# Zero products first, held loads and another x layout at the start of a decoder trunk

## The chip, the cores and the metric

The kernel runs on one core of a Trainium2 chip. The metric is device time in microseconds (us). A run's time is that of the whole execution; the profile of one execution also gives the span from its first to its last instruction.

## The reference

A trunk of two decoder layers in float32 on an input x of 256 tokens by 1024 channels. The first layer mixes tokens with a gated MLP, the second with block attention; each is followed by a gated MLP with a causal convolution, and each of the four sublayers ends in `x <- LayerNorm(alpha * x + f(x))`. What matters here is the head of the first sublayer:

```python
def chunked_gmlp(x, w_in, ln_g, ln_b, w_s, b_s, w_out):
    z = jax.nn.gelu(x @ w_in)          # (256, 1024) @ (1024, 2048)
    u, v = jnp.split(z, 2, axis=-1)
    v = layer_norm(v, ln_g, ln_b)
    ...
    return (u * sv.reshape(B, S, GMLP_WIDTH)) @ w_out
```

The kernel begins with the v half: x times the right 1024 columns of `w_in`, which are stored as the input `a_v`.

## The kernel before, in words

Every product of matrices is made of products on TensorE of a 128x128 stationary operand with up to 512 moving columns, in the type fp32r. To keep float32 accuracy each operand is split in two: `hi`, the value rounded to fp32r (ScalarE, ACT, line 338), and `lo`, the rest (VectorE, DVE, line 344). Each product is then three: hi by hi, hi by lo, lo by hi (`rows_step`, line 553; the instruction is at line 326).

All weights come through one queue of loads that SyncE (SP) issues in order (`load`, line 353; the DMA instruction is at line 355). They are cut into chunks of 128 partitions by 2048 columns, 1 MB each, which land in two buffers in turn (`raws`). A chunk covers two k tiles of 128 rows of the weight. `prep` (line 385) loads a chunk and splits it into `whi` and `wlo` tiles of 1024 columns, five chunks ahead of TensorE. A chunk can only be loaded into a buffer when both splits of the chunk two places earlier have read it, so the third chunk waits for the splits of the first.

At the start there is nothing to run ahead of, so the first loads are cut up and their order on SP is set by ranks (`FIRST`, line 382; `XFIRST`, line 383). The program's tiles are called raw_85 and raw_86 in the listing of instructions. The pieces, with the names that this text uses:

| rank | load | size | name here |
|---|---|---|---|
| 0 | a_v chunk 0, columns 0 to 511 | 256 KB | W0a |
| 1 | x, k tile 0 | 128 KB | x0 |
| 2 | a_v chunk 0, columns 512 to 1023 | 256 KB | W0b |
| 3 | x, k tile 1 | 128 KB | x1 |
| 4 | a_v chunk 0, columns 1024 to 2047 | 512 KB | W0c |
| 5 | x, k tiles 2 and 3 | 256 KB | x23 |
| 6, 7 | a_v chunk 1, its two halves | 512 KB each | W1a, W1b |
| 8 | x, k tiles 4 to 7 | 512 KB | x47 |
| none | a_v chunks 2 and 3 | 1 MB each | W2, W3 |
| none | LayerNorm rows for v | 1 MB | lnrow |
| none | a_u chunk 0, the u half's first weights | 1 MB | U0 |

W0a to W0c hold k tiles 0 (W0a, W0b) and 1 (W0c); W1 holds 2 and 3, W2 holds 4 and 5, W3 holds 6 and 7. x is stored transposed, `xT`, with 128 partitions (`load_xt`, line 433); in its rows the token half t stands outside the k tile, so a load of n k tiles moves two pieces of n times 512 bytes per partition.

The v products (`gmlp`, line 641) go over k tiles 0 to 3 for both token halves and then over k tiles 4 to 7 for the first half and the second. A k tile for one token half is two column halves of 512, each with its own PSUM bank, with three products each. So the first four k tiles are 48 products, and the 49th and 50th are the first two that need W2: one with its `whi`, one with its `wlo`.

The order of all instructions is worked out when the program is built: operations are recorded, `Plan.emit` (line 122) gives each a due time from its followers, simulates the engines with estimated costs and writes each engine's stream out by the simulated start. TensorE's main stream keeps the recorded order. What a load waits for is put in by the framework: a buffer's last readers and writers.

Of the kernel before, what the change touches and what calls it, by code (L numbers as in the profile page):

```python
# [11 lines left out]
F32 = mybir.dt.float32  # L12
# [6 lines left out]
P = 128  # L19
D = 1024  # L20
S = 256
DEPTH = 2
KT = D // P
FFN = 2816
FT = FFN // P
NT = S // P
# [9 lines left out]
HALF = 512  # L36
CH = 2048
SUB = 1024
# [7 lines left out]
T1_WAITS = (2600, 3300, 4000, 4700)  # L46
REST = 25000, 9000, 25000
AHEAD = 12000


class Buf:
# [164 lines left out]
def flat(ap):  # L216
    n = 1
    for d in ap.shape[1:]:
        n *= d
    return n  # L220
# [3 lines left out]
def trunk_kernel(ctx: ExitStack, tc: tile.TileContext, a: dict, out: bass.AP):  # L224
    nc = tc.nc
    plan = Plan()
    sb = ctx.enter_context(tc.tile_pool(name="sb", bufs=1))
# [9 lines left out]
    raws = Ring(tiles("raw", RAWS, CH))  # L237
# [9 lines left out]
    rr = sb.tile([P, 2 * FT * S], F32R, name="rr")  # L247
# [28 lines left out]
    state = {"age": 0, "next": 0}  # L276

    def taken(i, long):
        old = bank_of[i][1]
# [34 lines left out]
                bank_of[i] = (bank_of[i][0], b, False)  # L314


    def mms(seq, r, w, fill=False):

        ns = 0.0
        for o, l, x, _, _ in seq:  # L320
            n = flat(x)
            ns += max(107.0, n / 2.4) + 2.5 if l.dtype == F32R else (218.0 if n <= P else n / 0.6 + 5)

        def emit():
            for o, l, x, start, stop in seq:
                nc.tensor.matmul(o, l, x, start=start, stop=stop)  # L326
        plan.op("pe", ns, emit, r, w, fill)

# [24 lines left out]
    def load(o, src, w, r=(), nbytes=None, rank=None):  # L353
        nbytes = nbytes or flat(o) * P * 4
        plan.op("sp", nbytes / 360.0, lambda: nc.sync.dma_start(o, src), r, w, nbytes=nbytes, rank=rank)  # L355

    def split(hi, lo, src, psum=False, by="act"):

# [21 lines left out]


    FIRST = {0: [(0, 512, 0), (512, 1024, 2), (1024, 2048, 4)], 1: [(0, 1024, 6), (1024, 2048, 7)]}
    XFIRST = ((0, 1, 1), (1, 1, 3), (2, 2, 5), (4, 4, 8))

    def prep(i):
        name, c = stream[i]
        raw = raws.new()
        cuts = FIRST.get(i, [(0, CH, None)])
        for s, e, rank in cuts:
            load(raw.ap[:, s:e], a[name][c, :, s:e], [(raw, range(s // 256, e // 256))], rank=rank)  # L390
# [15 lines left out]
    def sub(name, c, s):  # L406
        return chunks[where[name, c]][s]
# [18 lines left out]
    def xt_view(b):  # L426
        return b.ap

    xh, xl = xt_new()
    xT32 = place("ff", HALF, KT * S)  # L430
    xv32 = xT32.ap.rearrange("p (t k c) -> p t k c", t=NT, k=KT)

    def load_xt(k, n, rank):
        load(xv32[:, :, k:k + n, :], a["xT"][:, :, k:k + n, :], [(xT32, [(t, j) for t in range(NT) for j in range(k, k + n)])],
             rank=rank)
# [13 lines left out]
    def ln_rows(i):  # L449
        b = rowring.new()  # L450
        src = a["lnrow"]
        load(b.ap, bass.AP(tensor=src.tensor, offset=src.offset + i * 2 * D, ap=[[0, P], [1, 2 * D]]), [b])
        return b, b.ap.rearrange("p (a d) -> p a d", a=2)

    def load_mixer():
# [94 lines left out]
            plan.later(wait, lambda k0=k0: turn(k0))  # L550


    def rows_step(pieces, hk, lk, r, hi, lo, first, last):

        for o, n, b in pieces:
            parts = range(o // 256, (o + n) // 256)
            mms([(b.ap[:, :n], x, w.ap[:, o:o + n], first and j == 0, last and j == 2)
                 for j, (x, w) in enumerate([(hk, hi), (hk, lo), (lk, hi)])], r + [(hi, parts), (lo, parts)], [b])
        plan.tick()

    def cols_times(b, h, l, hi, lo):
# [21 lines left out]
    def project_out(name, nk, at, xold, li, rows_i):  # L583
# [23 lines left out]
        for t in range(NT):  # L607
# [33 lines left out]
    def gmlp():  # L641
        at = xt_at(xh, xl)
        pieces = [[(o, HALF, bank(True)) for o in (0, HALF)] for _ in range(NT)]
        order = [(k, t) for k in range(4) for t in range(NT)] + [(k, t) for t in range(NT) for k in range(4, KT)]
        v = []
        for k, t in order:
            rows_step(pieces[t], *at(k, t), *sub("a_v", k // 2, k % 2), k == 0, k == KT - 1)
            if t == NT - 1 and k % 2:
                spent("a_v", k // 2)
            if (k, t) == (3, NT - 1):  # L650
                rows = ln_rows(0)
                ws, bs = load_mixer()
            if k == KT - 1:
                vt = place("ff", HALF + t * D, D)
                for o, n, b in pieces[t]:
                    act(vt.ap[:, o:o + n], b.ap, AF.Gelu_apprx_tanh, [b], [(vt, range(o // S, (o + n) // S))],
                        psum=True, table="gelu")
                    done_with(b)
                st, mean, rstd = stats(vt, vt.ap, [(0, HALF), (HALF, HALF)])
                scaled(vt, vt.ap, st, mean, rstd, rows)  # L660
                v.append(vt)
# [17 lines left out]
        for g in range(GROUPS):  # L679
            b = bank()  # L680
# [12 lines left out]
    def conv_up(layer, h, l):  # L693
# [42 lines left out]
        for t in range(NT):  # L736
            b = half()
            for k in range(KT):
# [7 lines left out]
                plan.tick()  # L746
            plan.tick(AHEAD)
            y = yring.new()
# [11 lines left out]
    def moba(h, l, scr):  # L760
# [14 lines left out]
        for ks in (range(5), range(5, KT)):  # L775
            for t in range(NT):
# [4 lines left out]
                if ks[0] == 0 and t == 0:  # L781
                    plan.tick(AHEAD)
                if ks[0]:
# [97 lines left out]
    at = gmlp()  # L881
    h, l = project_out("a_out", KT, at, xtok, 0, 1)
    at = conv_up(0, h, l)
    scr = build_bias(10 * S)
    h, l = project_out("f_dn0", FT, at, xtok, 1, 2)
    at = moba(h, l, scr)
    h, l = project_out("b_o", KT, at, xtok, 2, 3)
    at = conv_up(1, h, l)
    project_out("f_dn1", FT, at, xtok, None, 4)
    plan.tick(1e9)  # L890
    plan.emit()


# [9 lines left out]
def _layout(i):  # L903
    f = lambda v: np.ascontiguousarray(np.asarray(v, dtype=np.float32))
# [65 lines left out]
```

## Time and profile before

| | before |
|---|---|
| time, median of 3 runs | 572.7 us (571.51 to 573.66) |
| time of the profiled execution | 571.2 us |
| its span | 569.5 us |
| TensorE products busy | 556.1 us, 98% of the span |
| VectorE, ScalarE busy | 464.3 us (82%), 359.2 us (63%) |
| moved by DMA | 110.92 MB, mean 195 GB/s |

The profiled execution is 1.7 us longer than its span. PE is TensorE's products, PEld its weight loads, DVE VectorE, ACT ScalarE, POOL GpSimd, SP SyncE. A busy share near 100% on PE says that products were always under way, not at which clock they ran; a product's own time in a row is longer than the distance to the next one, since products overlap in the array. The distance of the starts is what a product costs.

### The profile page before, as it was taken

Reading aid. Unit: us, or ns where it says so; the run is one execution under the profiler, and the core shown is the slowest. Engines: PE = TensorE matmul, PEld = TensorE weight load, DVE = VectorE, ACT = ScalarE, POOL = GpSimd, SP = SyncE. Lnnn points to the kernel's source line nnn. Section 1 sums busy time; section 2 is a strip of 40 time slices with the busy share of each in tenths; the row PEclk is TensorE's granted clock in tenths of the full one; section 3 lists DMA queues with packets and bytes.
Section 4 is the critical chain, followed back from the end, with each engine's and each line's share of the span. In section 5 each row is a group of like instructions: output and inputs, shape, how many; then the busy total and the mean of one; then the engine's idle time right before and its main releaser. Section 6 shows DMA issues by size and latency. Waiting matters only on the chain.

```text
span 569.5 us, 8289 instructions
## 1 busy us (share of the span) xinstructions
PE 556.1 (98%) x3098; PEld 474.9 (83%) x3098; DVE 464.3 (82%) x873; ACT 359.2 (63%) x652; POOL 11.5 (2%) x17
## 2 busy tenths in 40 slices
PE   6999999999999999999999999999999999999994
PEld 4799888888888878888888877788888888888884
DVE  5598989999999997467958988579989999996526
ACT  5555558776777686335578877377777767775300
POOL 0020010000000000001000000010000000000001
PEclk9999999999999999999999999999999999999998
DMA  7897435547554577742665653506455556566302
GB/s 266 330 361 283 181 146 182 189 153 279 171 211 155 216 229 266 270 165 74 222 221 185 194 210 115 222 2 221 156 218 219 201 174 218 195 242 229 147 1 74
DMA packets 20132, 110.92 MB, mean 195 GB/s; under 512 B 2251, under 2 KB 6268, under 8 KB 7676
## 3 DMA queue, kind: packets, MB, share of 16 engines
q1 hardware_dynamic: 20092, 110.39, 54.2%
q8 instruction: 24, 0.39, 0.3%
q14 instruction: 16, 0.13, 0.1%
HBM read 109.31 MB, written 1.07 MB: 194 GB/s over the span
## 4 chain that ended last, share of the span: by engine, by line
PE 95%; DMA 2%; DVE 1%; SPq 0%; ACT 0%; issue 0%; DVEq 0%
PE twos L326 52%; PE bank L326 41%; DMA raw<-in_a_v 2%; PE bank L332 1%; PE twos L332 1%; DVE wlo L344 0%; DVE x L348 0%; SPq L355 0%; ACT whi L338 0%; DVE stat L494 0%; DVEq L966 0%; DVE stat L497 0%; DVE stat L499 0%; DVE xt L344 0%
## 5 line engine op out<-in xcount | busy, mean ns | idle before, releaser
L344 DVE TENSOR_TENSOR wlo<-raw,whi 128x1024 fp32r<-128x1024 f32 (+1 forms) x212 | 228.2, 1099 | 33.7 <-ACT whi L338 32.8
L338 ACT ACTIVATE whi<-raw 128x1024 fp32r<-128x1024 f32 (+1 forms) x212 | 194.8, 954 | 55.1 <-DMA raw<-in_f_dn 21.3
L326 PE MATMUL twos<-xt,whi 128*128 128x512 f32 x640 | 222.2, 394 | 0.0
L326 PE MATMUL twos<-xt,wlo 128*128 128x256 f32 x640 | 177.3, 277 | 0.0
L326 PEld LDWEIGHTS twos<-xt,whi 128*128 128x128 f32 x640 | 120.0, 188 | 27.8
L326 PE MATMUL bank<-whi,rr 128*128 128x512 f32 x432 | 135.5, 391 | 0.0
L326 PEld LDWEIGHTS twos<-xt,wlo 128*128 128x128 f32 x640 | 120.1, 188 | 0.1
L326 PEld LDWEIGHTS bank<-whi,rr 128*128 128x128 f32 x432 | 81.1, 188 | 17.9 <-issue 1.0
L326 PE MATMUL bank<-wlo,rr 128*128 128x512 f32 x216 | 84.0, 389 | 0.0
L326 PE MATMUL bank<-xt,whi 128*128 128x256 f32 (+1 forms) x256 | 71.0, 348 | 0.0
L348 DVE SCALAR_TENSOR_TENSOR ff<-ff,convc 128x254 f32<-128x254 f32 (+1 forms) x160 | 69.6, 478 | 0.3
L338 ACT ACTIVATE ff<-twos 128x512 f32<-128x512 f32 (+1 forms) x56 | 30.8, 565 | 47.9 <-PE twos L326 44.8
L326 PE MATMUL bank<-xt,wlo 128*128 128x256 f32 x192 | 54.0, 281 | 0.0
L326 PEld LDWEIGHTS bank<-xt,whi 128*128 128x128 f32 x256 | 44.0, 190 | 6.8 <-issue 1.0
L326 PEld LDWEIGHTS bank<-wlo,rr 128*128 128x128 f32 x216 | 40.6, 188 | 8.0
L338 ACT ACTIVATE ff<-ff,convc 128x256 f32<-128x256 f32 x80 | 45.6, 592 | 1.9 <-DVE ff L344 1.2
L344 DVE TENSOR_TENSOR ff<-twos,ff 128x512 f32<-128x512 f32 (+1 forms) x48 | 30.9, 645 | 15.3 <-ACT ff L338 13.0
L326 PE MATMUL twos<-whi,xt 128*128 128x512 f32 x128 | 42.1, 396 | 0.0
L338 ACT ACTIVATE ff<-bank,lncol 128x128 f32<-128x128 f32 x48 | 18.8, 458 | 29.1 <-PE bank L332 29.1
L326 PEld LDWEIGHTS bank<-xt,wlo 128*128 128x128 f32 x192 | 36.4, 190 | 0.0
L348 DVE SCALAR_TENSOR_TENSOR x<-x,bank 128x512 f32<-128x512 f32 x16 | 11.0, 686 | 25.0 <-PE bank L326 25.0
L326 PEld LDWEIGHTS twos<-whi,xt 128*128 128x128 f32 x128 | 24.1, 188 | 4.8
(71 smaller groups left out, 489.1 us busy)
## 6 DMA issues: line engine op xcount, KB each, us to landing
raw<-in_f_up SPq DMA_DIRECT2D x44, 1024.0 KB, 4.8
raw<-in_f_dn SPq DMA_DIRECT2D x22, 1024.0 KB, 4.9
raw<-in_b_qk SPq DMA_DIRECT2D x8, 1024.0 KB, 4.9
lnrow<-in_lnrow SPq DMA_DIRECT2D x5, 1024.0 KB, 6.7
raw<-in_a_u SPq DMA_DIRECT2D x4, 1024.0 KB, 5.1
raw<-in_a_out SPq DMA_DIRECT2D x4, 1024.0 KB, 5.0
raw<-in_b_v SPq DMA_DIRECT2D x4, 1024.0 KB, 4.9
raw<-in_b_o SPq DMA_DIRECT2D x4, 1024.0 KB, 5.0
```

The source lines that it names most:

```text
L326: nc.tensor.matmul(o, l, x, start=start, stop=stop)
L332: nc.tensor.transpose(o, x, ident.ap)
L338: plan.op("act", ns, lambda: nc.scalar.activation(o, x, func, **kw), r, w, table=table)
L344: dve(70 + 1.04 * flat(x), lambda: nc.vector.tensor_tensor(o, x, y, op=op), r, w)
L348: lambda: nc.vector.scalar_tensor_tensor(o, x, s, y, op0=op0, op1=op1), r, w)
```

## The change

Four things change, all at the start of the program.

1. After the plan is made and before its instructions are written out, VectorE clears 512 columns of the tile `rr` (which is first used much later), and TensorE multiplies them eight times into a PSUM bank that nothing has used yet (`WARM = 8`).
2. Three loads get a hold: `load` first issues a transfer of 16 numbers from a tile that an earlier load fills into a scratch row. It reads what that load writes, so SP waits for its landing, and everything behind it on SP waits too. x23 is held until W0a has landed, W1b until W0c has, and lnrow until W3 has.
3. `xT` is stored with the k tile outside the token half, so that a load of n k tiles is one piece of n times 1024 bytes per partition.
4. The 12 products of k tile 0 are issued together, sorted by column half first, and inside it hi by hi, x's lo by hi, hi by W's lo, each for both token halves.

```diff
@@ mms @@
         def emit():
-            for o, l, x, start, stop in seq:
+            if into is not None and not ready:
+                return
+
+            for o, l, x, start, stop in seq if into is None else [q for _, _, q in sorted(into, key=lambda q: q[:2])]:
                 nc.tensor.matmul(o, l, x, start=start, stop=stop)
@@ load @@
+        def emit():
+            for j, (i, at) in enumerate(holds):
+                k = state["held"] = state["held"] + 16
+                nc.sync.dma_start(scratch[:, k:k + 16], loaded[i].ap[:1, at:at + 16])
...
+            if len(holds) < 2:
+                nc.sync.dma_start(o, src)
+        plan.op("sp", nbytes / 360.0, emit, r, w, nbytes=nbytes, rank=rank)
@@ prep, load_xt, ln_rows @@
+    HOLD = {5: [(0, 0)], 7: [(0, SUB)]}
+    scratch = sb.tile([1, 128], F32, name="scratch")
+    loaded = {}
...
-    xv32 = xT32.ap.rearrange("p (t k c) -> p t k c", t=NT, k=KT)
+    xv32 = xT32.ap.rearrange("p (k t c) -> p t k c", t=NT, k=KT)
...
+             holds=[(3, 0)] if i == 0 else ())
@@ rows_step @@
+            if into is not None:
+                into += [(i, (0, 2, 1)[j], q) for j, q in enumerate(seq)]
+            mms(seq, r + [(hi, parts), (lo, parts)], [b], into=into, ready=into is not None and len(into) == 12)
@@ trunk_kernel, end @@
+    zeros = rr[:, :HALF]
+    nc.vector.memset(zeros.bitcast(F32), 0.0)
+    for _ in range(WARM):
+        nc.tensor.matmul(banks[-1], zeros[:, :P], zeros, start=True, stop=True)
     plan.emit()
@@ _layout @@
-        "xT": f(x.reshape(NT, P, KT, P).transpose(3, 0, 2, 1)),
+        "xT": f(x.reshape(NT, P, KT, P).transpose(3, 2, 0, 1).reshape(P, KT * S)),
```

SP at the start of the program, before: the loads of the table above in the order of their ranks, then W2, W3, lnrow and U0.

```order
L355 DMA raw_85<-in_a_v 128x512
L355 DMA ff<-in_xT 128x2x128
L355 DMA raw_85<-in_a_v 128x512
L355 DMA ff<-in_xT 128x2x128
L355 DMA raw_85<-in_a_v 128x1024
L355 DMA ff<-in_xT 128x2x256
L355 DMA raw_86<-in_a_v 128x1024 x2
L355 DMA ff<-in_xT 128x2x512 [waits DMAHW0_49]
L355 DMA raw_85<-in_a_v 128x2048 [waits DMAHW2_49,DMAHW4_49,DMAHW1_49,DVE_49]
L355 DMA raw_86<-in_a_v 128x2048 [waits DMAHW7_49,DMAHW6_49,DVE_49]
L355 DMA lnrow_90<-in_lnrow 128x2048 [waits DMAHW3_49]
L355 DMA raw_85<-in_a_u 128x2048 [waits DMAHW1_49,DVE_49]
```

The same place after. DMAHW0 to 7 are eight semaphores that the loads take in turn, so a wait on one is a wait for the landing of an earlier load.

```order
L370 DMA raw_85<-in_a_v 128x1024
L366 DMA scratch<-raw_85 1x16x1 [waits DMAHW0_49]
L370 DMA ff<-in_xT 128x512
L370 DMA raw_86<-in_a_v 128x1024
L366 DMA scratch<-raw_85 1x16x1 [waits DMAHW4_49]
L370 DMA raw_86<-in_a_v 128x1024 [waits DMAHW1_49]
L370 DMA ff<-in_xT 128x1024 [waits DMAHW2_49]
L370 DMA raw_85<-in_a_v 128x2048 [waits DMAHW3_49,DMAHW5_49,DMAHW0_49,DVE_49]
L370 DMA raw_86<-in_a_v 128x2048 [waits DMAHW7_49,DMAHW1_49,DVE_49]
L366 DMA scratch<-raw_86 1x16x1 [waits DMAHW4_49]
L370 DMA lnrow_90<-in_lnrow 128x2048 [waits DMAHW6_49]
L370 DMA raw_85<-in_a_u 128x2048 [waits DMAHW3_49,DVE_49]
```

No load has changed its place among the loads: three tiny transfers stand between them now, each with a wait. W2 also waits for the two tiny transfers that read its buffer (DMAHW5 and 0).

TensorE at the start, before. bank_107 and bank_108 are the column halves of the first token half, bank_109 and bank_110 those of the second; whi_65 and wlo_75 are k tile 0 of the weights.

```order
L326 MATMUL bank_107<-whi_65,xt 128x512
L326 MATMUL bank_107<-wlo_75,xt 128x512
L326 MATMUL bank_107<-whi_65,xt 128x512
L326 MATMUL bank_108<-whi_65,xt 128x512
L326 MATMUL bank_108<-wlo_75,xt 128x512
L326 MATMUL bank_108<-whi_65,xt 128x512
L326 MATMUL bank_109<-whi_65,xt 128x512
```

And after:

```order
L924 MATMUL twos_106<-rr 128x512 x8
L330 MATMUL bank_107<-whi_65,xt 128x512
L330 MATMUL bank_109<-whi_65,xt 128x512
L330 MATMUL bank_107<-whi_65,xt 128x512
L330 MATMUL bank_109<-whi_65,xt 128x512
L330 MATMUL bank_107<-wlo_75,xt 128x512
L330 MATMUL bank_109<-wlo_75,xt 128x512
L330 MATMUL bank_108<-whi_65,xt 128x512
```

Eight products of zeros stand ahead, and the first product with a `wlo` is the fifth instead of the second. Behind k tile 0 TensorE's order is as before, and so are the orders of ScalarE, of GpSimd and, apart from the new clearing at its head, of VectorE.

## Rows read from the trace of the kernel before

**Rows 1.** The page of the profile: busy time, share of the span and instructions of each engine.

```profile
PE 556.1 (98%) x3098; PEld 474.9 (83%) x3098; DVE 464.3 (82%) x873; ACT 359.2 (63%) x652; POOL 11.5 (2%) x17
```

**Rows 2.** The chain that ended last, in order of time: start and length in us, and what it was (the number of instructions behind the x).

```profile
3.15 5.63 DMA raw<-in_a_v
...
8.80 0.64 ACT whi L338
...
10.79 7.21 DMA raw<-in_a_v
...
18.03 1.07 ACT whi L338
...
19.12 1.24 DVE wlo L344
...
20.40 19.62 PE bank L326 x119
...
561.94 0.43 DVE x L348
```

**Rows 3.** TensorE's own waits over the whole span: who waited for whom, us in total, times, longest.

```profile
PE bank L326 <- DVE xt L361: 4.9, 1, 4.9
PE bank L326 <- DVE wlo L344: 0.8, 1, 0.8
```

**Rows 4.** TensorE's products in order of time: start us, us, what, how many in a row, and idle time before. A row of x2 is two products.

```profile
4.92 0.77 PE L326 MATMUL bank<-whi,xt 128*128 128x512 f32 x1 [4.92 <-DVE xt L361]
5.77 0.80 PE L326 MATMUL bank<-wlo,xt 128*128 128x512 f32 x1
...
8.50 0.63 PE L326 MATMUL bank<-wlo,xt 128*128 128x512 f32 x1
...
9.78 0.63 PE L326 MATMUL bank<-wlo,xt 128*128 128x512 f32 x1
10.20 0.98 PE L326 MATMUL bank<-whi,xt 128*128 128x512 f32 x2
11.03 0.40 PE L326 MATMUL bank<-wlo,xt 128*128 128x512 f32 x1
...
17.87 0.39 PE L326 MATMUL bank<-wlo,xt 128*128 128x512 f32 x1
...
18.55 0.39 PE L326 MATMUL bank<-wlo,xt 128*128 128x512 f32 x1
18.78 0.86 PE L326 MATMUL bank<-whi,xt 128*128 128x512 f32 x2
20.40 0.50 PE L326 MATMUL bank<-wlo,xt 128*128 128x512 f32 x1 [0.76 <-DVE wlo L344]
...
31.46 0.28 PE L326 MATMUL bank<-xt,wlo 128*128 128x256 f32 x1
```

**Rows 5.** SP's issues of loads in order of time: start us, us from the first to the end of the last of the row.

```profile
0.80 0.38 SPq L355 DMA_DIRECT2D raw<-in_a_v  x1
...
3.79 0.55 SPq L355 DMA_DIRECT2D ff<-in_xT  x1
4.38 1.07 SPq L355 DMA_DIRECT2D raw<-in_a_v  x2
...
10.79 3.79 SPq L355 DMA_DIRECT2D raw<-in_a_v  x2
14.63 0.43 SPq L355 DMA_DIRECT2D lnrow<-in_lnrow  x1
```

**Rows 6.** Five stretches of the start: length, busy time of each engine with its instructions, granted clock, share of the DMA engines' time, GB/s.

```profile
1.80:5.00 3.20, 0.08 (x1) 0.11 (x1) 0.45 (x3) 0.91 (x2) 0.00 (x0) 1.00 0.70 211
5.00:8.80 3.80, 3.72 (x8) 2.63 (x9) 2.10 (x6) 1.14 (x3) 0.00 (x0) 1.00 0.82 252
8.80:13.50 4.70, 4.70 (x17) 3.71 (x17) 3.83 (x7) 4.07 (x8) 0.00 (x0) 1.00 1.03 393
13.50:18.00 4.50, 4.50 (x22) 3.72 (x21) 1.99 (x4) 1.15 (x2) 0.00 (x0) 1.00 0.96 333
18.00:20.50 2.50, 1.74 (x8) 0.92 (x6) 1.38 (x2) 2.01 (x2) 0.00 (x0) 1.00 1.04 436
```

**Rows 7.** The same view of the rest of the span.

```profile
20.40:561.90 541.50, 541.50 (x3049) 463.92 (x3049) 450.49 (x843) 348.87 (x635) 9.88 (x10) 1.00 0.54 193
```

**Rows 8.** The DMA view of the first 12 us: GB/s in 40 slices of 0.3 us, and one kind of load with its size and its median time from issue to landing.

```profile
GB/s 0 0 0 0 0 0 130 184 179 196 174 299 357 249 230 179 118 207 282 358 348 294 229 254 113 195 212 260 287 375 393 413 437 423 437 376 423 396 376 430
...
raw<-in_a_v SPq DMA_DIRECT2D x2, 256.0 KB, 3.4
```

**Rows 9.** VectorE in order of time, in the same columns as rows 4.

```profile
0.87 0.06 DVE L421 MEMSET nhalf<- 128x1 f32 x1 [0.87 <-PEq L963]
...
5.03 0.68 DVE L344 TENSOR_TENSOR wlo<-raw,whi 128x512 fp32r<-128x512 f32 x1
...
27.38 2.36 DVE L344 TENSOR_TENSOR wlo<-raw,whi 128x1024 fp32r<-128x1024 f32 x2 [0.75 <-ACT whi L338]
...
34.64 0.74 DVE L348 SCALAR_TENSOR_TENSOR ff<-ff,stat,lnrow 128x512 f32<-128x512 f32 x1
```

**Rows 10.** ScalarE in order of time.

```profile
4.21 0.63 ACT L338 ACTIVATE whi<-raw 128x512 fp32r<-128x512 f32 x1 [2.13 <-DMA raw<-in_a_v]
...
26.29 2.01 ACT L338 ACTIVATE whi<-raw 128x1024 fp32r<-128x1024 f32 x2 [0.38 <-DMA raw<-in_a_u]
```

More of the change, by code (lines that the diff above doesn't have):

```diff
@@ L48 @@
 AHEAD = 12000
+WARM = 8
 class Buf:
@@ L275, in trunk_kernel @@
     bank_of = [(i - BANKS, None, False) for i in range(BANKS)]
-    state = {"age": 0, "next": 0}
+    state = {"age": 0, "held": -16}
     def taken(i, long):
@@ L314, in done_with, with mms @@
                 bank_of[i] = (bank_of[i][0], b, False)
-    def mms(seq, r, w, fill=False):
+    def mms(seq, r, w, fill=False, into=None, ready=False):
         ns = 0.0
@@ L351, in ts, with load @@
         dve(187 + 0.52 * flat(x), lambda: nc.vector.tensor_scalar(o, x, s1, s2, op0=op0, op1=op1), r, w)
-    def load(o, src, w, r=(), nbytes=None, rank=None):
+    def load(o, src, w, r=(), nbytes=None, rank=None, holds=()):
         nbytes = nbytes or flat(o) * P * 4
-        plan.op("sp", nbytes / 360.0, lambda: nc.sync.dma_start(o, src), r, w, nbytes=nbytes, rank=rank)
+        n = flat(o) // max(1, len(holds))
+        def emit():
+            for j, (i, at) in enumerate(holds):
+                k = state["held"] = state["held"] + 16
+                nc.sync.dma_start(scratch[:, k:k + 16], loaded[i].ap[:1, at:at + 16])
+                if len(holds) > 1:
+                    nc.sync.dma_start(o[:, j * n:(j + 1) * n], src[:, j * n:(j + 1) * n])
+            if len(holds) < 2:
+                nc.sync.dma_start(o, src)
+        plan.op("sp", nbytes / 360.0, emit, r, w, nbytes=nbytes, rank=rank)
     def split(hi, lo, src, psum=False, by="act"):
@@ L386, in prep @@
         name, c = stream[i]
-        raw = raws.new()
+        raw = loaded[i] = raws.new()
         cuts = FIRST.get(i, [(0, CH, None)])
         for s, e, rank in cuts:
-            load(raw.ap[:, s:e], a[name][c, :, s:e], [(raw, range(s // 256, e // 256))], rank=rank)
+            load(raw.ap[:, s:e], a[name][c, :, s:e], [(raw, range(s // 256, e // 256))], rank=rank,
+                 holds=HOLD.get(rank if rank is not None else (i, s), ()))
         subs = []
@@ L430, in trunk_kernel @@
     xT32 = place("ff", HALF, KT * S)
-    xv32 = xT32.ap.rearrange("p (t k c) -> p t k c", t=NT, k=KT)
+    xv32 = xT32.ap.rearrange("p (k t c) -> p t k c", t=NT, k=KT)
     def load_xt(k, n, rank):
-        load(xv32[:, :, k:k + n, :], a["xT"][:, :, k:k + n, :], [(xT32, [(t, j) for t in range(NT) for j in range(k, k + n)])],
-             rank=rank)
+        sl = slice(k * S, (k + n) * S)
+        load(xT32.ap[:, sl], a["xT"][:, sl], [(xT32, [(t, j) for t in range(NT) for j in range(k, k + n)])], rank=rank,
+             holds=HOLD.get(rank, ()))
         for t in range(NT):
@@ L451, in ln_rows @@
         src = a["lnrow"]
-        load(b.ap, bass.AP(tensor=src.tensor, offset=src.offset + i * 2 * D, ap=[[0, P], [1, 2 * D]]), [b])
+        load(b.ap, bass.AP(tensor=src.tensor, offset=src.offset + i * 2 * D, ap=[[0, P], [1, 2 * D]]), [b],
+             holds=[(3, 0)] if i == 0 else ())
         return b, b.ap.rearrange("p (a d) -> p a d", a=2)
@@ L550, in ln_back, with rows_step @@
             plan.later(wait, lambda k0=k0: turn(k0))
-    def rows_step(pieces, hk, lk, r, hi, lo, first, last):
-        for o, n, b in pieces:
+    def rows_step(pieces, hk, lk, r, hi, lo, first, last, into=None):
+        for i, (o, n, b) in enumerate(pieces):
             parts = range(o // 256, (o + n) // 256)
-            mms([(b.ap[:, :n], x, w.ap[:, o:o + n], first and j == 0, last and j == 2)
-                 for j, (x, w) in enumerate([(hk, hi), (hk, lo), (lk, hi)])], r + [(hi, parts), (lo, parts)], [b])
+            seq = [(b.ap[:, :n], x, w.ap[:, o:o + n], first and j == 0, last and j == 2)
+                   for j, (x, w) in enumerate([(hk, hi), (hk, lo), (lk, hi)])]
+            if into is not None:
+                into += [(i, (0, 2, 1)[j], q) for j, q in enumerate(seq)]
+            mms(seq, r + [(hi, parts), (lo, parts)], [b], into=into, ready=into is not None and len(into) == 12)
         plan.tick()
@@ L645, in gmlp @@
         v = []
+        into = []
         for k, t in order:
-            rows_step(pieces[t], *at(k, t), *sub("a_v", k // 2, k % 2), k == 0, k == KT - 1)
+            rows_step(pieces[t], *at(k, t), *sub("a_v", k // 2, k % 2), k == 0, k == KT - 1, into if k == 0 else None)
             if t == NT - 1 and k % 2:
```

## The prediction, on record before the result

> **What bounds the kernel now.** I began with the page: products busy 98% of the span [rows 1], so the time is what TensorE has to do, plus the places where it waits, plus its pace. Second, its waits: it waits twice in the whole span, 4.9 us for the first data and 0.8 us at one place soon after [rows 3]. Third, the chain of waits: from 20.40 on it is TensorE, up to the last normalization at 561.94 [rows 2], and the stretch 20.4 to 561.9 has 541.50 us of products in 541.50 us [rows 7]. So whatever happens before 20.40 moves the end one for one, as long as later data keep up. Fourth, what ends at 20.40: the chain goes back through the splits of W2 on VectorE and ScalarE (18.03 to 20.36), W2's load (issued 10.79, landed 18.00), the splits of W0c that free the buffer (8.80 to 10.79) and W0c's load (issued 3.15, landed 8.78) [rows 2]. The head is bound by loads.
>
> TensorE is close behind them. Its products of 512 columns come every 1.28/3 = 0.427 us early on (8.50 to 9.78) and every 0.68/3 = 0.227 us later (17.87 to 18.55) [rows 4]. 512 columns in 0.427 us is the lower of the clock's two levels, 1.2 GHz; the later pace, 0.227 us, fits 2.4 GHz only. The granted clock of these stretches reads 1.00 throughout [rows 6], so here the level is read from the starts. It rises between the pair that starts at 10.20 and the product at 11.03, some 6.0 us after the first product at 4.92, and TensorE was busy nearly all of that time. 13 products ran at the low level. The 48th and 49th are the pair from 18.78; the 50th, the first that needs W2's lo, starts at 20.40 [rows 4]. Earlier data alone, or a faster pace alone, would each gain little: both have to move.
>
> **Part by part: the zero products.** Clearing 128x512 numbers has no row. From below it is the 0.06 us of the clearing of one column, from above the 0.68 us of a subtraction over 512 columns [rows 9]. I take 0.5, as it writes as many columns as the latter and reads none. It starts at 0.87, when VectorE has nothing else until the first x has landed after 4.2, and the products start at about 1.45. Eight of them at 0.427 are 3.4 us: the last one makes room at 4.87. The first real product came at 4.92, held by x and W0a (ScalarE starts on W0a at 4.21 and takes 0.63 [rows 10]). So I count nothing for them and put the first real one at 4.95; were the clearing 0.68 and the first start slower by the 0.35 us that the very first product takes above its neighbours' pace (0.77 against 0.427), it would be 5.4. TensorE is then busy from 1.45 on, and with the same 6.0 us the clock rises at 7.45. Until then 6 products at 0.427 instead of 13: the 50th stands at 4.95 + 6 x 0.427 + 43 x 0.227 = 17.3, if data are there. Bounds: a clock that is up when the first real product comes gives 4.95 + 49 x 0.227 = 16.1, one that rises as late as before (13 low) 4.95 + 13 x 0.427 + 36 x 0.227 = 18.7.
>
> **The order of k tile 0.** The same 12 products. The first lo product waited in the old order: it starts at 5.77, 0.85 us behind the first product at 4.92 [rows 4], where 0.427 is the pace. In the new order the four products ahead of it fill that hole. It is worth 0.4 us, and is already in the 17.3, which has no hole.
>
> **Holds and layout: when W0c lands.** Up to the end of W0c 1.31 MB have to come. The DMA engines moved 211 GB/s from 1.8 to 5.0 and 252 up to 8.8 [rows 6], in all 1.63 MB: 0.32 MB of it were x23 and W1, which were issued at 3.79 and 4.38 [rows 5] and share with W0c. The first hold keeps them back until W0a has landed at about 4.2. At the same rates 1.31 MB are there at 5.0 + (1.31 - 0.675)/0.252 = 7.5; at the 393 GB/s of the stretch with larger pieces [rows 6], 5.1. The layout makes 128 pieces of 1 KB out of 256 of 512 bytes in x0 and x1. I take 7.2, near the rate that this stretch had. The Trainium skill (DMA: Bandwidth & Descriptors, section Specifications) puts the smallest transfer for line rate at 512 bytes, so by it the layout gives nothing on the wire; W0c then lands at 7.5 and everything below comes 0.3 later. No run here shows it apart yet.
>
> **W2.** From W0c's landing to W2's issue took 2.0 us of splits (8.80 to 10.79 [rows 2]): 9.2 now. On SP three issues stand between, the second tiny one, W1b and x47, at 0.33 to 0.72 us each (nearest rows 0.38 to 0.55 [rows 5]): 7.2 + 1.6 = 8.8, so they hide in the splits. What has to land by then is 4.19 MB, 2.88 MB after W0c; at 393 GB/s that is 7.3 us, and W2 is there at 14.5. In the run before the same sum gives 15.6 (3.48 MB by 13.5, the rest at 333 GB/s), but W2 landed at 18.00, 2.4 us late, with W3 (second of the pair issued from 10.79 to 14.58) and lnrow (14.63) on the same queue [rows 5]. The third hold takes lnrow out, W3 stays. So W2 lands between 14.5 and 16.9. TensorE needs 2.4 us from landing to the 50th product (18.00 to 20.40): 16.9 to 19.3. I take 14.5, because the hold removes one of the two that share and the queue has fewer loads in it. Then 16.9 is ahead of TensorE's own 17.3, and TensorE sets the place: 20.40 - 17.3 = 3.1 us gained.
>
> **What is late next.** W3 lands 2.5 us behind W2 as now (436 GB/s [rows 6] for 1 MB), and TensorE asks for each k tile of it 1.36 us later than for the one before, so it follows. lnrow waits for it until 17.0, and U0, 1 MB behind lnrow, for W2's splits: issue 18.0, and on the wire lnrow to about 21.0, U0 to 23.5, so that it lands near 23.9 instead of 26.27 [rows 10]. Its first lo is used at 31.46 and made by 28.6 (27.38 plus half of 2.36) [rows 4, 9]: 2.9 us of slack, of which 3.1 - 2.4 = 0.7 goes. lnrow itself is used at 34.6 [rows 9], over 10 us after it lands. Nothing further on waits, so 3.1 us reach the end.
>
> **The sum.** 571.2 us of the profiled execution - 3.1 = 568.1. That execution lies 1.5 below the median of the runs, 572.7, and I forecast medians: 569.6. What a measurement of this kernel can tell from no change is about 0.5%, 2.9 us, so the forecast sits on that line.
>
> **Rivals.** *W2 is still late* (its 2.4 us of sharing stay, as W3 was enough for them): the 50th product at 19.3, gain 1.1, 571.6. For it: W3 is not held. Against: it was issued at 14.25 at the earliest, and W2 has 1 MB that should be nearly through then.
>
> *The zeros don't lift the clock* earlier: 18.7, gain 1.7, 571.0. For it: only the one rise at 11 us is in the trace. Against: what stood before that rise was nothing but products.
>
> *Given back further on*: lnrow and U0, which now follow each other, both meet a lag as W2 did, 2.4 each. U0 lands at 28.7, 2.4 later than now, and 3.1 + 2.4 - 2.9 of slack = 2.6 us are lost again: 572.2. Against: it takes two lags, and nothing waits after 20.40 now.
>
> *The holds empty the queue*, and the kernel gets slower. Bytes come 1.0 us after an issue (issued at 0.80, first bytes at 1.8 [rows 5, 8]) and the issue itself takes 0.4 to 0.6, so where nothing else is queued a hold costs some 1.5 us of DMA time. If the first two both do, W2 lands at 17.5, and with the sharing of 2.4 at 19.9: the 50th product at 22.3, 1.9 us later than now, 574.6. It decides from a landing of W2 after 18.0 on. Against: while SP waits for W0a, x0 to W0c are queued, and while it waits for W0c, x23 and W1a, 0.79 MB or 2.0 us at 393 GB/s. The Trainium skill (DMA: Bandwidth & Descriptors, section Anatomy of one DMA) gives for the GpSimd path a fixed cost of about 2.0 us for each DMA, most of it the receipt that the last byte has landed, which speaks against waiting for a landing before the next issue: two such gaps would be 4.0 us, W2 at 18.5, 20.9 with the sharing, and the 50th product at 23.3, 575.6. The 3.4 us from issue to landing of a 256 KB load [rows 8] agrees with a large fixed part.
>
> **How the numbers follow.** Forecast 0.55, with its own range 568.3 to 570.8 from the bounds on the clock's rise (16.1 to 18.7 at the 50th product, its far ends less likely). W2 late 0.22, zeros in vain 0.09, given back 0.08, emptied queue 0.06. Faster by over 0.5% means below 569.8: six tenths of the first case and little of the others, 0.39. Slower by over 0.5% is above 575.6: the far end of the last case, 0.04. The rest, 0.57, is within 0.5%. The range runs from 568.2, most of the early rise, to 572.4, which takes in late W2, the zeros in vain and the loss further on.
>
> **What would show it.** In the new profile: eight products from about 1.45 at 0.427; the first real one by 5.0; the step to 0.227 near 7.5; W0c's split starting at 7.2 and W2's at 14.5 instead of 18.03; no wait of TensorE before its 50th product at 17.3; U0's split near 24, and no new wait after that. The forecast is wrong if W2's split starts after 15, if the step comes at 9 or later, or if TensorE waits again for U0 or later weights.

## The result, and the profile after

| | before | after |
|---|---|---|
| median of 14 runs each | 571.8 us (569.84 to 573.66) | 574.35 us (from 573.07) |

The ratio is 1.0053, with a 95% interval of 1.0038 to 1.0067: 0.5% slower. 569.6 was forecast, with 568.2 to 572.4 as its range, so the sign is wrong as well. One of the 14 executions after, the profiled one, took 3173 us, with 512-column products every 1.3 us from end to end, and is left out of the ratio (the other 13 have a median of 573.83 us). The profile after is therefore that of the same kernel, unaltered, in the first experiment (e1): 573.65 us with a span of 571.9.

TensorE's waits, who for whom, us in total, times, longest:

```profile
PE bank L330 <- DVE wlo L348: 2.0, 4, 0.8
PE twos L924 <- DVE nhalf L443: 1.5, 1, 1.5
PE twos L330 <- DVE ff L352: 1.0, 1, 1.0
PE bank L330 <- ACT whi L342: 0.6, 1, 0.6
```

Before, there were two waits, 4.9 for the first data and 0.8 at the 50th product [rows 3]. The first one is now 1.5, since TensorE starts on zeros. The rest has grown from 0.8 to 3.6, and one wait, on VectorE's `ff`, is of a kind that was not there.

TensorE in order of time:

```profile
1.52 3.75 PE L924 MATMUL twos<-rr 128*128 128x512 f32 x8 [1.52 <-DVE nhalf L443]
5.10 1.37 PE L330 MATMUL bank<-whi,xt 128*128 128x512 f32 x4
6.30 0.63 PE L330 MATMUL bank<-wlo,xt 128*128 128x512 f32 x2
6.77 1.08 PE L330 MATMUL bank<-whi,xt 128*128 128x512 f32 x4
7.69 0.63 PE L330 MATMUL bank<-wlo,xt 128*128 128x512 f32 x2
8.23 0.49 PE L330 MATMUL bank<-whi,xt 128*128 128x512 f32 x1
8.96 0.50 PE L330 MATMUL bank<-wlo,xt 128*128 128x512 f32 x1 [0.23 <-DVE wlo L348]
...
18.59 0.50 PE L330 MATMUL bank<-whi,xt 128*128 128x512 f32 x1 [0.57 <-ACT whi L342]
19.85 0.50 PE L330 MATMUL bank<-wlo,xt 128*128 128x512 f32 x1 [0.76 <-DVE wlo L348]
```

The first of the 12 products of k tile 0 starts at 5.10 and the 13th at 8.23; the four from 6.77 take (7.69 - 6.77)/4 = 0.23 us each, which is the higher of the two clock levels. That part of the forecast came true, even earlier than said. The 50th product, the first that needs W2's `lo`, was forecast for 17.3 and comes at 19.85 (20.40 before [rows 4]): it still waits for W2.

The chain of waits up to 42.3:

```profile
2.66 4.87 DMA raw<-in_a_v
...
7.54 0.50 SPq L366
...
8.09 5.68 DMA raw<-in_a_v
...
15.78 4.79 DMA raw<-in_a_v
...
20.59 1.07 ACT whi L342
...
21.68 2.37 DVE wlo L348 x2
...
24.07 8.42 DMA raw<-in_a_u
...
33.60 0.07 DVE wlo L348
...
36.89 4.81 DMA raw<-in_a_u
...
41.78 0.49 DVE ff L352
...
42.31 0.94 PE twos L330 x6
```

Before, TensorE was the chain from 20.40 on [rows 2]. Now loads and the splits behind them hold it up to 36.9, and a tiny transfer (line 366, the second hold) is part of it: behind it stands W1b (issued 8.09, landed 13.77), whose split frees the buffer for W3 (issued 15.78, landed 20.56), whose split frees it for U1 (issued 24.07, landed 32.49). The load in the last part of the chain (36.89 to 41.69) is not what TensorE waits for: from 36.78 on VectorE works without a pause, and from the `stat` row at 36.78 to the `ff` at 41.78 it needs 5.00 us, as it did before (32.55 to 37.55). SP's issues and the DMA rate show the rest, first SP:

```profile
7.54 0.50 SPq L366 DMA_DIRECT2D scratch<-raw  x1
...
10.64 5.46 SPq L370 DMA_DIRECT2D raw<-in_a_v  x2
20.58 0.50 SPq L366 DMA_DIRECT2D scratch<-raw  x1
21.13 0.58 SPq L370 DMA_DIRECT2D lnrow<-in_lnrow  x1
21.82 2.58 SPq L370 DMA_DIRECT2D raw<-in_a_u  x2
```

Then stretches in the columns of rows 6 (the last number is GB/s):

```profile
5.00:7.50 2.50, 2.50 (x11) 1.70 (x11) 1.79 (x6) 1.03 (x3) 0.00 (x0) 1.00 0.89 306
7.50:10.40 2.90, 2.67 (x11) 1.75 (x10) 2.23 (x6) 1.88 (x4) 0.00 (x0) 1.00 0.81 227
10.40:13.80 3.40, 3.40 (x15) 2.57 (x15) 1.33 (x3) 1.16 (x3) 0.00 (x0) 1.00 0.93 312
...
20.60:22.20 1.60, 1.60 (x8) 1.29 (x8) 0.85 (x2) 1.60 (x2) 0.00 (x0) 1.00 0.01 0
22.20:30.00 7.80, 7.75 (x35) 6.08 (x34) 2.54 (x3) 2.29 (x4) 0.00 (x0) 1.00 1.00 390
```

lnrow is issued at 21.13 instead of 14.63 [rows 5], 0.7 us ahead of U0. For 1.6 us nothing moves at all, and then lnrow's 1 MB stands in front of U0 and U1. ScalarE and VectorE show when these land and what is behind them:

```profile
29.98 2.01 ACT L342 ACTIVATE whi<-raw 128x1024 fp32r<-128x1024 f32 x2 [4.28 <-DMA raw<-in_a_u]
```

```profile
31.07 2.36 DVE L348 TENSOR_TENSOR wlo<-raw,whi 128x1024 fp32r<-128x1024 f32 x2 [4.64 <-ACT whi L342]
33.60 3.25 DVE L348 TENSOR_TENSOR wlo<-raw,whi 128x1024 fp32r<-128x1024 f32 x2 [0.17 <-ACT whi L342]
36.78 1.87 DVE L518 BATCH_NORM_STATS2 stat<-ff 128x6 f32<-128x512 f32 x3
...
38.86 0.74 DVE L352 SCALAR_TENSOR_TENSOR ff<-ff,stat,lnrow 128x512 f32<-128x512 f32 x1
...
41.78 0.48 DVE L352 SCALAR_TENSOR_TENSOR ff<-ff,stat,lnrow 128x256 f32<-128x256 f32 x1
```

The last of these rows before, and TensorE in the profile after:

```profile
37.55 0.48 DVE L348 SCALAR_TENSOR_TENSOR ff<-ff,stat,lnrow 128x256 f32<-128x256 f32 x1
```

```profile
40.84 0.42 PE L330 MATMUL twos<-ff 128*128 128x128 f32 x2
42.31 0.94 PE L330 MATMUL twos<-ff 128*128 128x128 f32 x6 [1.04 <-DVE ff L352]
```

U0 is there at 29.98 instead of 26.29 [rows 10] and its `lo` is begun at 31.07 instead of 27.38 [rows 9]. VectorE works in order: the normalization of v stands behind U1's split and starts at 38.86 instead of 34.64 [rows 9], 4.2 us later. The last piece that TensorE needs of it comes as late, at 41.78 instead of 37.55. The first two products with the normalized v (`twos`) still start without a wait, at 40.84; the third, the 171st in all, waits for that piece and starts at 42.31.

The start of a given product in the profiles, counted without the zero products, tells where time is won and lost. Each column is one execution; the other columns are the experiments e6, e2, e4 and e13 of the next section.

| product | before | changed (e1) | third hold only | without holds | zeros only | W2's own buffer |
|---|---|---|---|---|---|---|
| 13th (W0c) | 10.63 | 8.23 | 10.77 | 8.59 | 9.29 | 10.69 |
| 50th (W2) | 20.40 | 19.85 | 20.74 | 19.13 | 19.56 | 19.20 |
| 97th (U0) | 31.23 | 31.09 | 31.95 | 31.55 | 30.39 | 29.86 |
| 171st (normalized v) | 40.08 | 42.31 | 42.99 | 40.51 | 39.24 | 38.66 |
| 500th | 92.35 | 94.95 | 95.64 | 93.15 | 91.83 | 90.98 |

### The profile page after: what moved, and what is told of

The parts are those of the page before. It is cut to its first block, busy times and chain, and to the rows that moved or that the text cites. A ratio compares the mean times of both kernels' runs of the same rounds, so it can differ in the third digit from the quotient of the medians.

```text
span 3171.3 us, 8308 instructions
## 1 busy us (share of the span) xinstructions
PE 3162.3 (100%) x3106; PEld 2402.6 (76%) x3106; DVE 470.6 (15%) x874; ACT 364.0 (11%) x652; POOL 10.6 (0%) x17
## 4 chain that ended last, share of the span: by engine, by line
PE 100%; DVE 0%; issue 0%; DVEq 0%
PE twos L330 53%; PE bank L330 44%; PE bank L336 1%; PE twos L336 1%; PE twos L924 0%; DVE x L352 0%; DVE rr L922 0%; DVE stat L518 0%; DVEq L1000 0%; DVE stat L521 0%; DVE stat L523 0%; DVE nhalf L443 0%
## 5 line engine op out<-in xcount | busy, mean ns | idle before, releaser
L330 PE MATMUL twos<-xt,whi 128*128 128x512 f32 x640 | 1084.7, 1695 | 0.0
L330 PEld LDWEIGHTS twos<-xt,whi 128*128 128x128 f32 x640 | 584.7, 914 | 258.8 <-issue 258.8
L330 PE MATMUL twos<-xt,wlo 128*128 128x256 f32 x640 | 661.2, 1033 | 0.0
L330 PE MATMUL bank<-whi,rr 128*128 128x512 f32 x432 | 656.5, 1697 | 0.0
L330 PEld LDWEIGHTS twos<-xt,wlo 128*128 128x128 f32 x640 | 586.1, 916 | 0.8 <-issue 0.8
L330 PEld LDWEIGHTS bank<-whi,rr 128*128 128x128 f32 x432 | 392.9, 909 | 180.7 <-issue 179.9
L330 PE MATMUL bank<-wlo,rr 128*128 128x512 f32 x216 | 365.9, 1694 | 0.0
L330 PE MATMUL bank<-xt,whi 128*128 128x256 f32 (+1 forms) x256 | 331.3, 1385 | 0.0
L330 PEld LDWEIGHTS bank<-xt,whi 128*128 128x128 f32 x256 | 216.2, 913 | 55.6 <-issue 55.6
L330 PE MATMUL twos<-whi,xt 128*128 128x512 f32 x128 | 200.6, 1722 | 0.0
```

## The experiments

Each was timed beside the kernel before on one chip; "ratio" is to that kernel, with its 95% interval. Single profiles differ by a load's chance lateness (last section), so the verdicts go by the ratios. The profiled executions of e4 and e9 lie 1.6 and 1.7 us below the medians of their kernels.

**The changed kernel again, and two of its parts taken out.** e1 is unaltered. e2 takes out the three holds:

```diff
-    HOLD = {5: [(0, 0)], 7: [(0, SUB)]}
+    HOLD = {}
-             holds=[(3, 0)] if i == 0 else ())
+             holds=())
```

e3 takes out the clearing and the eight products of zeros, and e4 adds them alone to the kernel before.

> The changed kernel, unaltered, for a profile at TensorE's normal pace (the one at hand has a product of 512 columns every 1.3 us from end to end, and only its loads can be read). It is to be 2 to 3 us slower than before (574.35 against 571.8 in 14 runs each). Theory A, the clock is lost: the zero products raise the clock early, TensorE then outruns the loads, waits for W1b (landed 13.8 in the profile at hand) and W2 (18.0), the clock falls in a wait, and products run at 0.427 us again some time after 8 us; the 50th product then stands at 20.4 as before and the end is later by the number of low-paced products after it, some 12 for 2.5 us. Theory B, loads: TensorE keeps its pace, but a new wait of 2 to 3 us stands where U0 (landed 28.5 instead of 26.3) or lnrow is first used, near 31 us. Theory C, neither: the 50th product itself comes 2 to 3 us later than 20.4.

> The changed kernel without its three tiny transfers; zero products, layout and the order of k tile 0 stay. Theory A (the clock falls in waits for loads): still slower than before by 1 us or more, unless loads come so much earlier that no wait is left. Theory B (held loads come late): no slower than before, 570 to 572, with U0 landing at 26.3 or earlier. If W2 lands before 18.0 here, the holds cost what the layout gave.

> The changed kernel without the zero products and their clearing; holds, layout and order stay. Theory A: the loss is gone, 571 to 572, since the clock rises at about 11 us as before and TensorE has no long wait after it. Theory B: as slow as the changed kernel, 574 to 575. With W2 landing at 18.0 in both, the 50th product is at 20.4 in all of them.

> The kernel before with the eight zero products alone. Theory A: slower than before by 2 us or more, with low-paced products after a wait near 8 to 20 us. Theory B: as before, 571 to 573, with a longer wait of TensorE ahead of its 50th product and no other difference.

Measured: e1 574.05 us, ratio 1.0054 (1.0022 to 1.0086). e2 571.64, 1.0006 (0.9989 to 1.0023). e3 574.87, 1.0066 (1.0034 to 1.0098). e4 572.27, 1.0013 (0.9993 to 1.0032). So the loss comes with the holds and goes with them. The zero products neither lose nor win time that could be told, although in e2 and e4 the 50th product is 1.3 and 0.8 us early. In the profile of e2 this is given back at once: W3 lands at 21.1, and its `hi` and `lo` hold TensorE at the next two places.

```profile
16.76 2.00 ACT L342 ACTIVATE whi<-raw 128x1024 fp32r<-128x1024 f32 x2 [2.40 <-DMA raw<-in_a_v]
21.11 2.00 ACT L342 ACTIVATE whi<-raw 128x1024 fp32r<-128x1024 f32 x2 [2.35 <-DMA raw<-in_a_v]
```

W2's split now begins at 16.76, 1.3 earlier than before, but W3's at 21.11, 0.6 later than its 20.52. In the profile of e4, where W3 landed at 19.89, the gain is not given back (its 500th product is 0.5 us early); why the median of e4 gains nothing is not shown.

**Which hold.** e5 is the changed kernel without the third hold, e6 the kernel before with nothing but the third, e7 the changed kernel with the first hold alone, e8 the kernel before with the layout of x and the order of k tile 0 alone.

```diff
-             holds=[(3, 0)] if i == 0 else ())
+             holds=())
```

> The changed kernel without its third hold (lnrow goes to the queue behind W3 again, without waiting for it). Theory D, the third hold is the price: lnrow moves back into the hole of the queue between W3 and U0, U0 lands at 26 to 27 instead of 30.0, the waits at the first u products and at 41 us go, and the time is 570.5 to 572, 2.5 us less than the changed kernel. Theory E, the first two holds are the price, by W1b and W3 that come late: still 573.5 or more, with U0 landing at 28 or later.

> The kernel before with the third hold alone. Theory D: 573 to 575, W2 and W3 landing as before at 18 and 20.5 and U0 at 28.5 to 30, with a new wait of TensorE at its first u products near 31 or at 41. Theory E: 571 to 572.3, as before.

> The changed kernel with its first hold alone (x23 behind W0a). If the second hold is what keeps W2 late (W2 waits for the tiny transfer that reads its buffer, and W1b and x47 start behind an empty queue), W2 is issued at about 9.7 and lands at 15.5 to 16.7 instead of 17.5, the 50th product stands at 18 to 19.1 instead of 19.85, and the time is 570 to 571.5. If W2's landing is set by the bytes alone, it lands at 17 to 18 here too and the time is 571 to 572.

> The x layout and the order of k tile 0 alone: no zero products and no hold. By the prediction's step on the layout W0c lands some 0.3 us or more earlier than 8.8, so 8.0 to 8.5, W2 follows by as much and the time is 571 to 571.5; by the rule of the smallest transfer for line rate the layout gives nothing and it lands at 8.8. In either case no slower than before.

Measured: e5 572.17, 1.0001 (0.9976 to 1.0027). e6 574.05, 1.0037 (1.0012 to 1.0061). e7 573.66, 1.0022 (0.9996 to 1.0048). e8 571.56, 0.9995 (0.9970 to 1.0020). The third hold costs 2 to 3 us added and taken away, so theory D holds. Its place is as in the changed kernel: in e6, TensorE waits 1.8 us for the normalized v, and these stretches stand around the tiny transfer that is issued at 21.48:

```profile
20.20:21.50 1.30, 0.76 (x3) 0.67 (x4) 1.30 (x2) 0.18 (x2) 0.00 (x0) 1.00 0.04 19
21.50:23.20 1.70, 1.70 (x9) 1.38 (x9) 0.94 (x2) 1.70 (x2) 0.00 (x0) 1.00 0.01 0
23.20:30.00 6.80, 6.69 (x30) 5.20 (x29) 2.44 (x3) 2.57 (x4) 0.00 (x0) 1.00 0.99 388
```

The first two holds cost nothing that could be told (e5 against e2), and bring nothing either. e7's interval leaves it open whether the first alone costs; in its profile TensorE waited at the 61st and 62nd product and then ran some seven products at 0.427 us, the lower level, until 28.1. The granted clock of that stretch reads 0.53 (third number from the end):

```profile
24.80:28.20 3.40, 3.40 (x10) 2.64 (x9) 0.78 (x2) 1.58 (x3) 0.00 (x0) 0.53 0.69 243
```

**What in the third hold.** Is it lnrow that stands in front of U0, or the wait wherever it stands? In e9, e6's kernel with the planner told that lnrow comes after W3's split, so that it puts wsT, bs, U0 and U1 first, the hold is behind U1. e10 is the changed kernel with the same line. e11 has no hold but lnrow behind U0's split.

```diff
+             r=[(chunks[3][0][0], range(4))] if i == 0 else (), hold=3 if i == 0 else None)
```

> The kernel before plus the third hold alone, as in the run with that hold only, but the planner is told that lnrow comes late (after W3's split), so that it puts two other 512 KB loads and then U0 and U1 behind W3, and the tiny transfer and lnrow behind U1. The hold is still there, with its wait (now for U1) and its issue. Theory D' (the price of the third hold is the hole in the queue behind W3 and lnrow standing in front of U0 and U1): U0 lands by 27 us, U1 by 29.5, no new wait of TensorE at 40 to 43 us, time as before, 571.3 (ratio 0.998 to 1.002). Rival D'' (the price is the gated issue itself, or lnrow's lateness): lnrow lands at about 31.5, VectorE's normalization of v is late again, time 573.5 to 574.5 (ratio 1.003 to 1.006).

> The changed kernel whole, with that same late lnrow: all three holds, zero products, layout and order of k tile 0 stay. D': U0 lands by 27 us and U1 by 30, the wait of TensorE near 42 us goes, and the time is that of the changed kernel without its third hold, 571.5 to 572.3 (ratio 1.000 to 1.002). D'': as the changed kernel, 574 (1.004 to 1.006).

> Zero products, layout and order of k tile 0, no holds at all, and lnrow told to come after the split of U0, so that it stands behind U1. If the head is bound by W2 and W3 alone, W2 lands at 16.7, W3 by 20.5 and U0 by 26, the 50th product comes at about 19 and the wait for W3 that the kernel without holds had is shorter by what lnrow took from W3: 570 to 571 (ratio 0.997 to 1.000). If W3's landing at 21 was a single slow DMA engine and not lnrow's share of the queue, the same 571.6 as without holds (1.000).

Measured: e9 572.61, 1.0020 (1.0002 to 1.0038). e10 573.76, 1.0040 (1.0026 to 1.0055). e11 572.09, 1.0005 (0.9991 to 1.0020): lnrow's later place without a wait costs nothing that could be told. D' as I had put it falls. U0 is early in the profiles of e9 and e10 (landed at 24.5 and 25.2), but e10 loses as much as e1. Its hole has only moved: in e10 the tiny transfer waits for U1 until 30.43, nothing moves from 30 to 32, and the next a_u and a_out weights come late instead. The profile of e9 has the same hole (0 GB/s from 28.7 to 30.3) and no wait of TensorE for the normalized v, so there the hole held up nothing that TensorE needed. TensorE's waits of e10 behind W3:

```profile
PE twos L330 <- DVE ff L352: 1.0, 1, 1.0
PE twos L330 <- DVE ff L348: 0.9, 1, 0.9
```

So the wait itself is left. e12 has the tiny transfer at the same place as e6, but reading x, which landed long ago; e6 and e12 differ in that wait alone.

```diff
-                nc.sync.dma_start(scratch[:, :16], loaded[hold].ap[:1, :16])
+                nc.sync.dma_start(scratch[:, :16], xT32.ap[:1, :16])
```

> The kernel before with the third tiny transfer in front of lnrow, but reading a piece of x that landed long ago, so that it holds nothing back: the only difference from the run with the third hold alone is the wait for W3's landing. If the wait makes the price (lnrow leaves the hole of the queue behind W3 and everything behind it on SP comes later), lnrow is issued at about 15.3 and the time is that of before plus at most 0.6 us of one more issue: 571.0 to 572.2 (ratio 0.999 to 1.002). If the tiny transfer itself is the price (its issue, its lane among the eight semaphores, 64 bytes on the queue): as with the hold, 573.5 to 574.3 (ratio 1.003 to 1.005).

Measured: 571.84, 1.0005 (0.9988 to 1.0022); lnrow is issued at 15.12, and the queue has no hole:

```profile
20.20:21.50 1.30, 1.30 (x8) 1.05 (x7) 0.66 (x1) 1.30 (x2) 0.00 (x0) 1.00 0.84 303
21.50:23.20 1.70, 1.64 (x8) 1.04 (x7) 1.70 (x2) 1.54 (x2) 0.00 (x0) 1.00 0.87 347
```

The intervals of e6 (from 1.0012) and e12 (up to 1.0022) touch, but all ten executions of e6 took 573.2 us or more, and ten of the twelve of e12 less (on two chips, with 570.88 and 571.22 us as medians of the kernel before). The wait is the price, and the transfer and its issue cost nothing that could be told.

**What binds the head.** W2 may only be issued when a buffer is free. In e13 it lands in columns of `ff` that are unused so early. Nothing else is changed in the program text, but the planner then puts U0 ahead of lnrow and orders VectorE and later loads somewhat differently. e14 adds the zero products, the layout and the order, e15 only the zero products, e16 only layout and order.

```diff
+    EARLY = {2: 2560}
+
+    def early(i):
+        return place("ff", EARLY[i], CH)
...
-        raw = raws.new()
+        raw = early(i) if i in EARLY else raws.new()
```

> The kernel before with one change: W2 lands in columns of the tile ff that nothing uses yet, instead of W0's buffer, so its issue waits for no split; W3 then takes W0's buffer and U0 takes W1's. No hold, no zero products. (The planner orders VectorE and the later loads somewhat differently for it.) Theory F (what binds the head is that W2 and W3 may only be issued when a buffer is free): W2 is issued at 7 instead of 10.8 and lands by 16, W3 by 18.5; TensorE, whose clock rises at 11 as before, reaches its 50th product at its own pace, 18.9 to 19.1, without waiting, 1.4 us earlier: 569.5 to 570.3 (ratio 0.996 to 0.998). Rival G (the bytes on the wire bind it, and more loads on the queue at once only make W0c and W1 later): W0c lands at 9.5 or later, the 50th product at 20 or later, 571 to 573 (ratio 1.000 to 1.003).

> The same buffer for W2 together with the zero products, the layout and the order of k tile 0, without any hold. Theory F: with data early the faster start of TensorE counts at last: the 50th product at 17.3 to 18.0 and no wait for W3, 568.5 to 569.5 (ratio 0.994 to 0.997). Rival G: W0c, W1 and W2 share the wire, TensorE waits at k tiles 1 and 2 instead, 570.5 to 572 (ratio 0.999 to 1.001).

Measured: e13 569.92 (569.49 to 571.26), 0.9973 (0.9961 to 0.9986); e14 571.89, 1.0003 (0.9987 to 1.0019). e13 is faster than both kernels, as theory F had it. Its first stretches, in the columns of rows 6:

```profile
8.80:13.50 4.70, 4.70 (x17) 3.78 (x17) 3.88 (x8) 4.02 (x8) 0.00 (x0) 1.00 1.04 411
13.50:18.00 4.50, 4.50 (x21) 3.72 (x21) 2.84 (x5) 3.12 (x4) 0.00 (x0) 1.00 1.02 430
```

430 GB/s instead of 333 from 13.5 to 18 [rows 6]. W2's split starts at 16.03 and W3's at 18.52, and TensorE does not wait again after its first data:

```profile
18.52 0.39 PE L326 MATMUL bank<-wlo,xt 128*128 128x512 f32 x1
18.75 0.61 PE L326 MATMUL bank<-whi,xt 128*128 128x512 f32 x2
19.20 0.39 PE L326 MATMUL bank<-wlo,xt 128*128 128x512 f32 x1
```

The 50th product, at 19.20, follows the 49th by 0.23. It is 1.2 us early, nearly the whole gain in time (1.3 us between the medians), which leaves little for the planner's other order. In e14 the zero products, the layout and the order added nothing to this gain: it was gone. Two more runs have them one by one.

> The kernel before with W2 in columns of ff (as the plain kernel with that buffer, 0.9973) and the zero products, nothing else of the change. Theory H (data early and pace early: TensorE's next limit is W0c, whose split feeds its 13th product): the 13th product moves from 10.7 to 9.5 at most, the 50th from 19.2 to 18.2, if W2 and W3 land by 16 and 18.5 as in the plain one: 568.9 to 569.9 (ratio 0.995 to 0.9975). Rival I (the zero products are what took the gain away in the kernel with all of them): 571 to 572.3 (ratio 0.9995 to 1.002).

> The kernel before with W2 in columns of ff and the new layout of x and order of k tile 0, without zero products. If the layout took the gain away (rival L: with its shorter issues x23 and W1 are on the queue earlier, beside W0c, and the sixteen DMA engines drift 3 us apart, so that every load lands with the last of them, as in the profile of the kernel with all of them, where W0c landed at 9.4 and W2 at 17.1): 571 to 572.3 (ratio 0.9995 to 1.002). If the zero products took it (I): as the plain one, 569.5 to 570.3 (0.9965 to 0.998).

Measured: e15 570.75, 0.9983 (0.9968 to 0.9997); e16 570.19, 0.9981 (0.9964 to 0.9997). Both lie between the two answers that had been written down, and neither differs from e13's 0.9973 or from the other beyond the intervals; which of the parts takes the gain in e14 stays open. What the profiles show is that W0c's split started at 9.44 in e14 and 9.94 in e16, 8.60 and 8.75 in e15 and e13, and that in e15 TensorE, 0.3 us ahead at the 50th product, waited again up to 39.8 and 53.5 for work of VectorE.

## Why the prediction was wrong, point by point

**The zero products, right.** They start at 1.52 (1.45 said), the last one makes room for the first real product at 5.10 (4.95 said), and the high pace came before 7.45. That the rival "the zeros don't lift the clock" would be the loss is out. That "the same 6.0 us" is a constant is wrong: the last product at the low pace, without zeros, started at 10.20 before, but at 7.67 in e12 and 9.09 in e9, whose starts are alike. With zeros it lay between none (e1, e2) and 6.93 (e4). The forecast also counted earlier data alone as worth little ("both have to move"); e13, which has earlier data alone, gained most, and only kernels with its buffer gained at all (e13, e15, e16).

**W0c, right.** 7.2 said, 7.54 in e1, and 7.4 to 8.2 in the other profiles with the first hold (8.78 before).

**W2, the first step that failed:** "2.88 MB after W0c; at 393 GB/s that is 7.3 us, and W2 is there at 14.5". It took from 7.52 to 17.46, 9.9 us, past my bound of 16.9. The 393 was the rate of a full queue. The second hold let go of W1b only at 8.09, when W1a and x23 were the only loads left on it, and 7.5 to 10.4 ran at 227 GB/s. W1b landed at 13.77 instead of 12.24, and W2's issue stood at 10.64, not 9.2: a tiny transfer that had read W2's buffer had to land first (SP waited 1.4 us for it, which the order of after shows and my sum left out). So of the rivals "the holds empty the queue" was the nearest for the first two holds. It was priced at 574.6 with W2 landing after 18.0; the loss came elsewhere.

**W3, "so it follows", the second.** I gave it 2.5 us behind W2 without a place for its issue, which waits for W1b's split. In e1 it was issued at 15.78 and landed 3.1 behind W2. In e2 it was issued at 13.95 and landed 4.3 behind, but fifteen of its sixteen landing marks stood by 19.01, 2.3 behind, and only the last one was late (last section). In the profiles of e2, e5, e7 and e8, W3 was the next limit, and the first 50 products' gain of 0.7 to 1.7 us was gone by the 62nd (23.29 to 23.80; before 23.29); in e4 and e12, where W3 landed by 19.9, 0.9 and 1.2 us of it were left.

**lnrow and U0, the third and the one that sets the sign: the forecast gave the third hold no cost in its sum.** I had lnrow issued at 17.0 and U0 at 18.0, on the 14.5 for W2, and U0 landing at 23.9. They were 21.13 and 21.82, and U0 landed at 29.96. Before, lnrow went through the queue while U0 waited for its buffer; held, it left that hole empty and took 1 MB of wire time where U0 needed it. I saw the rival "given back further on" (572.2), but counted the slack only to the first product with U0's `lo` at 31.46. The near deadline was on VectorE: U1's split stands ahead of v's normalization in VectorE's order, and 4.2 us of lateness there are 2.2 at the 171st product and 2.4 in the span (571.9 against 569.5). Not all of it need be the hold: of U1's sixteen landing marks fifteen stood by 31.06 and the last at 32.49, against 28.98 and 29.16 before, so that about 2.1 of its 3.3 us are the later place on the queue and the rest one late mark.

e12 against e6 shows that this price is the wait. e10, where lnrow's place was mended and the loss stayed, speaks for the hole and not just the place; but e9's 1.0020, with the same hole, says that part of it goes with the place. How the price divides between the two is not settled.

**The range.** The first case's own 568.3 to 570.8 does not follow from its bounds: 572.7 less gains of 4.3 and 1.7 is 568.4 to 571.0, and W2 at its stated 16.9 allowed no less than 569.2.

**The layout.** The Trainium skill (DMA: Bandwidth & Descriptors, section Specifications) would have 512-byte pieces at line rate already, so that pieces of 1 KB win nothing on the wire. No run here shows it apart. The time of e8, 0.9995, cannot decide it, since W3 held TensorE at the 62nd product there. Its stretch 5.0 to 8.8 had 322 GB/s against 252 before and W0c landed at 7.93 instead of 8.78, one profile each; but SP's issues of x are shorter as well (0.42 us for x0 instead of 0.64), so the loads were on the queue earlier.

## What to carry to other kernels

A load that waits for another one's landing leaves a hole in the queue, here 1.6 us with 0 GB/s, and moves every load behind it on the issuing engine. Whether that costs time depends on what is behind it: ask which in-order engine has work queued behind those loads, since the nearest deadline may be that of a third party. Where a head is bound by loads, look first for what keeps the issue back (here a buffer that must be read first): 1 MB of unused space for one load brought 0.27%, while a faster start of the engine brought nothing. A rate measured with a full queue may not be used for a stretch in which the change itself empties it.

## What the runs showed of the hardware that was not expected

A load has sixteen landing marks in the trace, as many as there are DMA engines, and what waits for it starts behind the last one. In many profiles one to three of the sixteen came late, for other loads each time. Of W2 in the kernel before, fourteen had landed by 15.97, and the last at 18.00 (its split began at 18.03); of W3 in e2, fifteen by 19.01 and the last at 21.08; of U1 in e10, fifteen by 28.99 and the last at 30.41. So about 2.0 of my 2.4 us of "sharing" with W3 and lnrow, from which W2's later bound was made, were such a lateness. In e11, e14 and e16, with the new layout and no holds, the sixteen marks of W0c lay over 3 us apart, and it landed at 10.2, 9.4 and 9.9; in e2 and e8, with the same layout, at 7.9. Why is open.

The tiny transfer takes 0.5 to 0.6 us of SP and lands 1.6 us after its issue on an empty queue (the third in e1) and up to 4.2 behind others (the first in e5), so that a hold has a price even for the buffer that it only reads.

At the start the granted clock read 1.00 in stretches in which products came at 0.427 us [rows 6], so the level had to be read from the starts. The trace tells why: its first entry of the clock stands at 10.97 us in the kernel before and at 5.11 in e1, where the pace changes from 0.427 (10.63 and 5.10 are the last starts ahead of it), and the view counts time without an entry as 1.00. Where there is an entry the reading holds: 0.53 in e7, from 24.8 to 28.2, again with products at 0.427.
